# A hybrid decoder layer: activations of the output projections loaded ahead, weights through four tiles, and a new share of dense products per step

## The chip, the cores and the metric

The kernel runs on one core of one Trainium2 chip. The metric is the device time of one launch in microseconds (us), as the median of several runs; lower is better. A second source is one profiled execution, whose trace gives the start and the length of each instruction on the engines: TensorE (PE, with its weight loads as PEld), VectorE (DVE), ScalarE (ACT), GpSimd (POOL) and SyncE (SP, which here only starts transfers).

## The reference

One decoder layer for 2048 tokens of width 1024 in float32. Two recurrent mixers work side by side on the columns of one input projection, their outputs go through one output projection, and a gated convolutional FFN follows.

```python
h = _rmsnorm(x, norm1_w[l])
proj = h @ w_in[l]                          # 2048 HGRN2 columns, 1792 RWKV-7 columns
hg_p, rw_p = proj[..., :HG_COLS], proj[..., HG_COLS:]
q_raw, f_raw, i_raw, g_raw = jnp.split(hg_p, 4, axis=-1)
o_hg = _hgrn2_mixer(q_raw, f_raw, i_raw, g_raw, lower_bounds[l], hg_norm_w[l])
rw_p = rw_p + (_token_shift(rw_p) - rw_p) * rw_shift_mu[l]
r, k, v, wd, ad, gd = jnp.split(rw_p, rw_split, axis=-1)
o_rw = _rwkv7_mixer(r, k, v, wd, ad, gd, ...)
x = x + jnp.concatenate([o_hg, o_rw], axis=-1) @ w_out[l]
x = x + _conv_ffn(_rmsnorm(x, norm2_w[l]), w_up[l], conv_w[l], conv_b[l], w_down[l])
```

HGRN2 has 4 heads of 128, RWKV-7 has 8 heads of 64; both carry a state from token to token. A final RMSNorm ends the layer.

## The kernel before

**Precision.** Each large product is made of three (`mm3`, L269 to 272): both operands are split into a rounded part and a rest, by a cast on ScalarE and a subtraction on VectorE (`split`, L250, for weights; `split_to`, L245, for activations), and the products part·part, part·rest and rest·part are added up.

**Phase 1** covers the input projection, both recurrences and three quarters of the output projection, up to about 1300 us of the trace. The tokens lie in four blocks of 512. Three generators are advanced by one loop when the program is built, and so write one interleaved program:

- `rw_stream` runs RWKV-7 in eight supers (`rw_super(nb, s_)`: block nb, four heads each, numbered here 0 to 7 as 2nb + s_). A super prepares its operands, solves a triangular system per chunk of tokens on VectorE (the tiles E, Ti; L811 to 813) and on TensorE (lv, ZT, RHS, UV), runs the recurrence over chunks and stores its output to DRAM as oT (L949). Its `done["rw1"]` counts prepared supers, whose inputs r, k, v have been read; `done["rw2"]` counts finished ones.
- `hg_stream` runs HGRN2 in sixteen units (`hg_unit(nb, j)`), each of which stores 128 rows of oT (L1089).
- `dense()` is the work that fills TensorE: a list of jobs. Per block there are 30 projections P of 128 columns (eight `mm3` each), and the three output projections O0, O1 and O2 (`out_block`), each of 64 `mm3`, for the blocks 0 to 2. O0 stands behind the projections of block 1, O1 behind those of block 2, O2 behind those of block 3. Block 3's own output projection stands at the start of phase 2 (L1208 to 1281, tile `wacc`).

A step of the loop advances each recurrence to its next `yield`, and then the dense list until it has used up a credit of TICK = 2000 ns, at 648 ns for a projection's `mm3` and 680 for an output projection's:

```python
            for key, g in (("r", rw_), ("h", hg_)):
...
            fill(TICK)
```

The engines run their instructions in the order written, each waiting for its inputs and for free tiles.

**An output projection** O works on 512 tokens in four quarters (i2: 256 tokens; dh: 512 output columns). A quarter has eight weight tiles of 128 by 512, and each serves two `mm3`. A weight tile is loaded by GpSimd's queue into `woraw` (a ring of four tiles, tag wraw), and is split into wh and wl (four tiles each, which the projections' weights share). The activations hh and hl are those of the whole block; O0 and O1 read them from oT in DRAM during their first quarter, one of eight rows of 128 before each weight tile, through two tiles `oraw` (tag sg). O2 has the first 256 tokens ready (`oh`, `ol`) and reads the second 256 in its third quarter. The residual input xh goes through the weight ring in one quarter and through sg in the others. During the last quarter of O0 and O1 the next projections' activations are split into hh and hl (`next_block`).

Before a projection's products, `load(i + 1)` starts the next projection's weights (two of the four split tiles), also if an O job comes in between.

The tags s0, s1 and s2 hold r, k and v of a super (two rows of 512 tokens each), tl holds the low-rank columns of a block.

Of the kernel before, what the change touches and what calls it, by code (L numbers as in the profile page):

```python
# [7 lines left out]
F32 = mybir.dt.float32  # L8
# [10 lines left out]
P = 128  # L19
T = 2048  # L20
D = 1024
KD = D // P
BLK = 512
NBLK = T // BLK
FF = 2816
NFF = FF // P
TICK = 2000.0
# [40 lines left out]
def tile_layer(ctx, tc, consts, x, norm1_w, w_in, hg_lb_logits, hg_norm_w, rw_shift_mu, rw_w0, rw_w2,  # L68
# [5 lines left out]
    dma, store = nc.sync.dma_start, nc.gpsimd.dma_start  # L74
# [171 lines left out]
    def split_to(hi, lo, src):  # L246
        c_ = S.copy(hi, src)
        return c_, V.tensor_sub(lo, src, hi.bitcast(F32))
# [25 lines left out]
    def phase1(c1):  # L274
# [31 lines left out]
        def stg(tag, name, bufs):  # L306
            return sp.tile([P, BLK], F32, tag=tag, name=name, bufs=bufs)
# [68 lines left out]
                ready[k] += 1  # L376
            return f

        def out_block(nb, oh=None, ol=None, then=None):


            for i2 in range(2):
                for dh in range(2):
                    accs = [bank("pj") for _ in range(2)]
                    for k in range(KD):
                        if i2 == 0 and dh == 0 and oh is None:
                            raw = stg("sg", "oraw", 2)
                            dma(raw, oT[nb][k * P:(k + 1) * P, :])
                            split_to(hh[:, k, :], hl[:, k, :], raw)
                        if i2 == 1 and dh == 0 and oh is not None:  # L390
                            raw = stg("sg", "oraw", 2)[:, 0:256]
                            dma(raw, oT[nb][k * P:(k + 1) * P, 256:512])
                            split_to(hh[:, k, 256:512], hl[:, k, 256:512], raw)
                        raw = wp.tile([P, 512], F32, tag="wraw", name="woraw", bufs=4)
                        wload(raw, w_out[0, k * P:(k + 1) * P, dh * 512:dh * 512 + 512])
                        wh, wl = split(wp, raw, [P, 512], "w", 4)
                        if k == KD - 2:
                            inputs = dh == 0 and (i2 == 0) == (oh is None)
                            xh = [wp.tile([P, BLK], F32, tag="wraw", name="xh", bufs=4) if inputs else
                                  stg("sg", "xh", 2) for _ in range(2)]  # L400
                            for q in range(2):
                                t0 = nb * BLK + (i2 * 2 + q) * P
                                dma(xh[q], x[0, t0:t0 + P, dh * 512:dh * 512 + 512])
                        for q in range(2):
                            is_ = slice((i2 * 2 + q) * P, (i2 * 2 + q + 1) * P)
                            lhs = ((hh[:, k, is_], hl[:, k, is_]) if oh is None or i2 == 1 else
                                   (oh[k // 4][:, k % 4, is_], ol[k // 4][:, k % 4, is_]))
                            mm3(accs[q], lhs, (wh, wl), k == 0, k == KD - 1)
                            if i2 == 1 and dh == 1 and q == 1:
                                next_block(then, k)  # L410
                            yield 680
                    for q in range(2):
                        V.tensor_add(xh[q], accs[q], xh[q])
                        r0 = (i2 * 2 + q) * P
                        (nc.gpsimd.dma_start if nb == NBLK - 2 and i2 and dh else dma)(
                            x1d[nb][r0:r0 + P, dh * 512:dh * 512 + 512], xh[q])
# [42 lines left out]
        def split_h(nb, k):  # L459

            src, w = rows[nb][:, :, k * P:(k + 1) * P], vec("n1", k)
            h4, l4 = (t_[:, k, :].rearrange("p (i t) -> p i t", i=4) for t_ in (hh, hl))
            act(h4, src, AF.Copy, scale=w)
            V.scalar_tensor_tensor(l4, src, w, h4.bitcast(F32), ALU.mult, ALU.subtract)

        def next_block(nb, k):

            if nb is not None and nb < NBLK:
                for k_ in ([k - 2] if 2 <= k < KD - 1 else [k - 2, k - 1, k] if k == KD - 1 else []):
                    split_h(nb, k_)  # L470

        def sum_load(m):

# [12 lines left out]
        def o_take(m):  # L486

            def f():
                if m == 0:
                    t_ = xp_.tile([P, 2, 2, 4, 256], F32R, tag="xt", name="ohl", bufs=1)  # L490
                    rows["O"] = [[t_[:, c, i] for i in range(2)] for c in range(2)]
                t_ = wp.tile([P, 2, 256], F32, tag="wraw", name="oraw", bufs=4)
                dma(t_, oT[2][2 * m * P:2 * (m + 1) * P, 0:256].rearrange("(k p) t -> p k t", p=P))
                ks = slice(2 * (m % 2), 2 * (m % 2) + 2)
                for i_ in split_to(rows["O"][0][m // 2][:, ks, :], rows["O"][1][m // 2][:, ks, :], t_):
                    tc.keep_in_program_order(i_)
            return f
# [24 lines left out]
        def dense():  # L522
# [36 lines left out]
            for m in range(2):  # L559
                extra += [(at[3] + 14 + 5 * m, ("E", sum_load(m))), (at[3] + 17 + 5 * m, ("E", sum_make(m)))]  # L560
            extra += [(at[3] + 25 + m, ("W", 2, o_take(m))) for m in range(4)]
            for i, jb in sorted(extra, key=lambda e: e[0], reverse=True):
                jobs.insert(i, jb)
            cols = [jb[1] for jb in jobs if jb[0] == "P"]
# [25 lines left out]
            for n, jb in enumerate(jobs):  # L590
                if jb[0] == "E":
                    jb[1]()
                    continue
                if jb[0] == "A":
                    if jb[1] == 0:
                        banks = spread()
                        ahead = transposed(four_tiles(rows[0]), "n1", lambda: next(banks), to_h)
                    continue
                if jb[0] == "T":
                    turns.append(jb[1])  # L600
                    continue
                if jb[0] in "OW":
                    while done["rw2"] < 2 * jb[1] + 2 or done["hg"] < 4 * jb[1] + 4:
                        yield None
                    if jb[0] == "W":
                        jb[2]()
                    else:
                        yield from (out_block(2, *rows["O"]) if jb[1] == 2 else out_block(jb[1], then=jb[1] + 2))
                    continue
                _, col, ev, cond, fin = jb  # L610
                while not cond():
                    yield None
                load(i)
                ws = loaded.pop(i)
                if i == 0:
                    next(ahead)
                    next(ahead)
                    constants()
                load(i + 1)
                i += 1  # L620
                acc = bank("pj")
                then = jobs[n + 1][1] if jobs[n + 1][0] == "A" else None
                for k in range(KD):
                    wh, wl = ws[k // 4]
                    next(ahead, None)
                    mm3(acc, (wh[:, k % 4, :], wl[:, k % 4, :]), (hh[:, k, :], hl[:, k, :]), k == 0, k == KD - 1)
                    aside = k in (1, 5) and len(turns) > 0
                    if aside:
                        turns.pop(0)()
                    if k == KD - 1:  # L630
                        ev(acc)
                        if fin is not None:
                            fin()
                    next_block(then, k)
                    yield 648 + 436 * aside

        def last_dma(nb):
# [18 lines left out]
        def rw_super(nb, s_):  # L656
# [208 lines left out]
            for e in range(2):  # L865
                r0, c0 = er0(e), col0(1, e)
                act(M[r0:r0 + 64, 0, 1, :, :, 0:64], quv[1][c0:c0 + 64, :, :, 0:64], AF.Copy)
            yield
            yield
            XH = tile_("XH", [2, 9, 64], "XH")  # L870
            V.tensor_copy(XH[:, :, 0, :], Xc[:, 2 * s_:2 * s_ + 2, :])
# [82 lines left out]
        def hg_unit(nb, j):  # L954
# [122 lines left out]
            act(sq, op, AF.Square)  # L1077
            hi, lo = (rp.tile([P, BLK], F32R, tag=tag, name="part") for tag in ("Sf", "VT"))
            split_to(hi, lo, sq)
            yield  # L1080
            yield
            ms = bank("hg")
            add_up(ms, ones, hi, lo)
# [29 lines left out]
        def fill(ns):  # L1113
            nonlocal credit
            credit += ns
            while alive["d"] and credit > 0:
                try:
                    c = next(dn_)
                except StopIteration:
                    alive["d"] = False  # L1120
                    return
                if c is None:
                    credit = 0.0
                    return
                credit -= c

        while any(alive.values()):
            for key, g in (("r", rw_), ("h", hg_)):
                if alive[key]:
                    try:  # L1130
                        next(g)
                    except StopIteration:
                        alive[key] = False
            fill(TICK)


    if "1" in stages:
# [498 lines left out]
```

## Time and profile before

| | us |
|---|---|
| median of 3 runs | 2635.08 |
| lowest and highest | 2632.3, 2636.21 |
| profiled execution | 2639.41 |
| its span in the trace | 2637.6 |

| engine | share of the span |
|---|---|
| PE | 97% |
| PEld | 78% |
| DVE | 75% |
| ACT | 52% |
| POOL | 14% |

In a row of the windows view stand a stretch (us from the span's start), its length, the busy time of each engine with its number of instructions, the granted TensorE clock as a share of full speed (PEclk), the mean busy share of the 16 DMA engines, and what they moved in GB/s. A row of the timeline has start, length, engine, line, operation, output<-inputs, and in brackets the idle time of the engine just before and what ended it. In a view of one tile a row has minimum, median and maximum duration in ns and the first and last start. A name such as `hh L247` is the tile and the line that wrote it; a split has its helper's line, wherever it is called from.

### The profile page before, as it was taken

The numbers are of one execution on the slowest core, as the hardware profiler recorded it, in microseconds if no ns is written. First come the engines' busy times: TensorE is split into PE (matmuls) and PEld (weight loads), VectorE is DVE, ScalarE is ACT, GpSimd is POOL, SyncE is SP. The second block draws the span as 40 slices with busy tenths as digits, with TensorE's granted clock in tenths as the row PEclk, the third lists the DMA queues.
The fourth block names the chain that finished last, engine by engine and source line by source line (L and its number), as shares of the span: only waits on it lengthen the run. The fifth ranks groups of instructions, "written<-read, shape, count | busy, mean of one in ns | idle before, by whom it ended". The sixth has DMA issues, their size and how long they took to land.

```text
span 2637.6 us, 51053 instructions
## 1 busy us (share of the span) xinstructions
PE 2545.3 (97%) x19467; PEld 2046.8 (78%) x19467; DVE 1968.2 (75%) x3744; ACT 1384.5 (52%) x2266; POOL 381.7 (14%) x686
## 2 busy tenths in 40 slices
PE   7999999989999899999899999999999999999998
PEld 6877777767777677777688888887888888888887
DVE  5878676775576765787678799987998887766556
ACT  5566454555446554355466754556554554545444
POOL 6433222212222122222100000000000000000000
PEclk9999999989999999999899999999999999999999
DMA  8846463545655566755574477746764554998655
GB/s 309 236 161 191 159 167 119 148 145 200 195 170 141 168 204 181 252 181 161 193 251 136 130 233 260 235 158 217 243 204 132 170 171 131 333 321 284 200 190 188
DMA packets 380298, 518.98 MB, mean 197 GB/s; under 512 B 114463, under 2 KB 211093, under 8 KB 380053
## 3 DMA queue, kind: packets, MB, share of 16 engines
q1 hardware_dynamic: 325521, 337.38, 40.3%
q0 software_dynamic: 54464, 178.32, 20.9%
q8 instruction: 153, 2.51, 0.4%
q14 instruction: 92, 0.75, 0.1%
q10 hardware_dynamic: 68, 0.02, 0.0%
HBM read 372.99 MB, written 134.22 MB: 192 GB/s over the span
## 4 chain that ended last, share of the span: by engine, by line
PE 53%; issue 7%; DVE 6%; DMA 5%; ACT 4%; POOL 1%; SPq 0%; DVEq 0%; POOLq 0%; ACTq 0%
PE ua L270 5%; PE ua L272 5%; PE ua L271 5%; PE pj L270 3%; PE da L271 3%; PE da L270 3%; PE da L272 3%; PE ud L271 3%; PE pj L271 3%; PE ud L270 3%; PE ud L272 3%; PE pj L272 3%; PE db L271 2%; PE db L272 2%; PE db L270 2%
## 5 line engine op out<-in xcount | busy, mean ns | idle before, releaser
L270 PE MATMUL pj<-hh,wh 128*128 128x512 f32 x960 | 394.6, 411 | 8.2 <-issue 3.4
L272 PE MATMUL pj<-hh,wl 128*128 128x512 f32 x960 | 378.3, 394 | 0.0
L271 PE MATMUL pj<-hl,wh 128*128 128x512 f32 x960 | 377.7, 394 | 0.0
L270 PE MATMUL ua<-Bh,uwh 128*128 128x512 f32 x704 | 276.6, 393 | 2.3 <-ACT m L122 1.2
L272 PE MATMUL ua<-Bh,uwl 128*128 128x512 f32 x704 | 274.9, 391 | 0.0
L271 PE MATMUL ua<-Bl,uwh 128*128 128x512 f32 x704 | 274.5, 390 | 0.0
L270 PEld LDWEIGHTS pj<-hh,wh 128*128 128x128 f32 x960 | 181.2, 189 | 56.6 <-issue 10.1
L272 PEld LDWEIGHTS pj<-hh,wl 128*128 128x128 f32 x960 | 180.8, 188 | 41.0 <-issue 2.0
L271 PEld LDWEIGHTS pj<-hl,wh 128*128 128x128 f32 x960 | 181.5, 189 | 34.6 <-issue 1.6
L254 ACT CAST uwh<-uraw 128x512 fp32r<-128x512 f32 x220 | 134.5, 617 | 131.2 <-PE ua L271 54.7
L255 DVE TENSOR_TENSOR dal<-draw,dah 128x512 fp32r<-128x512 f32 x138 | 95.3, 691 | 108.3 <-ACT dah L254 106.9
L255 DVE TENSOR_TENSOR uwl<-uraw,uwh 128x512 fp32r<-128x512 f32 x220 | 147.4, 686 | 34.1 <-ACT uwh L254 33.8
L254 ACT CAST dah<-draw 128x512 fp32r<-128x512 f32 x138 | 85.7, 621 | 160.8 <-PE da L271 75.9
L270 PEld LDWEIGHTS ua<-Bh,uwh 128*128 128x128 f32 x704 | 132.4, 188 | 32.0 <-ACT m L122 3.8
L272 PEld LDWEIGHTS ua<-Bh,uwl 128*128 128x128 f32 x704 | 132.4, 188 | 27.9 <-DVE uwl L255 0.4
L271 PEld LDWEIGHTS ua<-Bl,uwh 128*128 128x128 f32 x704 | 132.3, 188 | 26.9
L1506 POOL DMA_DIRECT2D gd<-y x2 | 1.1, 542 | 948.8 <-DVE y L1504 948.8
L270 PE MATMUL ud<-Bh,uwh 128*128 128x512 f32 x352 | 138.2, 393 | 0.0
L272 PE MATMUL ud<-Bh,uwl 128*128 128x512 f32 x352 | 137.3, 390 | 0.0
L271 PE MATMUL ud<-Bl,uwh 128*128 128x512 f32 x352 | 137.2, 390 | 0.0
L271 PE MATMUL da<-dbl,dah 128*128 128x512 f32 x332 | 129.6, 390 | 0.3 <-DVE dbl L255 0.3
L272 PE MATMUL da<-dbh,dal 128*128 128x512 f32 x332 | 129.4, 390 | 0.0
(582 smaller groups left out, 6226.7 us busy)
## 6 DMA issues: line engine op xcount, KB each, us to landing
uraw<-in_w_up_dram SPq DMA_DIRECT2D x176, 256.0 KB
woraw<-in_w_out_dram POOLq DMA_DIRECT2D x96, 256.0 KB, 3.5
br<-gd SPq DMA_DIRECT2D x88, 256.0 KB
draw<-Sg SPq DMA_DIRECT2D x88, 256.0 KB
draw<-Tw SPq DMA_DIRECT2D x88, 256.0 KB
gd<-y SPq DMA_DIRECT2D x86, 256.0 KB
Sg<-br SPq DMA_DIRECT2D x72, 256.0 KB
xt<-x1d SPq DMA_DIRECT2D x32, 512.0 KB
```

What stands on the lines that cost most here:

```text
L254: S.copy(hi, src)
L255: V.tensor_sub(lo, src, hi.bitcast(F32))
L270: TE.matmul(acc, lh, rh, start=first, stop=False, skip_group_check=skip)
L271: TE.matmul(acc, lh, rl, start=False, stop=False, skip_group_check=skip)
L272: TE.matmul(acc, ll, rh, start=False, stop=last, skip_group_check=skip)
L1506: (dma if end is None else nc.gpsimd.dma_start)(gd_[2 * h + b][fb * P:(fb + 1) * P, :], ys[0][:, b * BLK:(b + 1) * BLK])
```

## The change

Four things change.

1. A new job "L" stands before the last projection ahead of O0 and of O1. `o_load` starts the loads of all eight rows of oT: six in pairs into the tiles s0, s1, s2, one into tl, one into sg. `next_out` splits them into hh and hl behind the products of that last projection, as soon as the projection has used the old ones (`behind(k)`). For O2, `o_half` loads the second 256 tokens into s0 and s1, and they are split in the second quarter and not in the third.
2. The projection ahead of an O job doesn't load the next projection's weights any more. O0 and O1 do so themselves, behind k = 3 of their last quarter (`ahead`). Until then all four split tiles take O's weights. xh always goes through sg.
3. The credit of a loop step is multiplied by 1.5 while super 3 or 5 lies between its preparation and its end (`done["rw1"]` 4 or 6), by 0.9 once all RWKV-7 inputs of the last block are projected, and else by 1.
4. The last super and the last two HGRN2 units have one `yield` less each.

The number of products, splits and weight loads is as before.

```diff
-        def out_block(nb, oh=None, ol=None, then=None):
+        def out_block(nb, oh=None, ol=None, then=None, ahead=None):
...
-                        if i2 == 0 and dh == 0 and oh is None:
-                            raw = stg("sg", "oraw", 2)
-                            dma(raw, oT[nb][k * P:(k + 1) * P, :])
-                            split_to(hh[:, k, :], hl[:, k, :], raw)
-                        if i2 == 1 and dh == 0 and oh is not None:
-                            raw = stg("sg", "oraw", 2)[:, 0:256]
-                            dma(raw, oT[nb][k * P:(k + 1) * P, 256:512])
-                            split_to(hh[:, k, 256:512], hl[:, k, 256:512], raw)
+                        if i2 == 0 and dh == 1 and oh is not None:
+                            split_to(hh[:, k, 256:512], hl[:, k, 256:512], rows["O2"][k // 4][:, k % 4, :])
...
-                            inputs = dh == 0 and (i2 == 0) == (oh is None)
-                            xh = [wp.tile([P, BLK], F32, tag="wraw", name="xh", bufs=4) if inputs else
-                                  stg("sg", "xh", 2) for _ in range(2)]
+                            xh = [stg("sg", "xh", 2) for _ in range(2)]
...
                             if i2 == 1 and dh == 1 and q == 1:
                                 next_block(then, k)
+                                if k == 3 and ahead is not None:
+                                    ahead()
...
+        def behind(k):
+            return [k - 2] if 2 <= k < KD - 1 else [k - 2, k - 1, k] if k == KD - 1 else []
...
+        def o_load(nb):
+            pieces = []
+            for u in range(3):
+                t_ = sp.tile([P, 2, BLK], F32, tag=f"s{u}", name="opair")
+                dma(t_, oT[nb][2 * u * P:2 * (u + 1) * P, :].rearrange("(k p) t -> p k t", p=P))
+                pieces += [t_[:, 0], t_[:, 1]]
+            for tag, bufs in (("tl", 1), ("sg", 2)):
+                pieces.append(stg(tag, "oraw", bufs))
+                k = len(pieces)
+                dma(pieces[-1], oT[nb][(k - 1) * P:k * P, :])
+            rows[("P", nb)] = pieces
+
+        def o_half(nb):
+            rows["O2"] = []
+            for u in range(2):
+                t_ = sp.tile([P, 4, 256], F32, tag=f"s{u}", name="ohalf")
+                dma(t_, oT[nb][4 * u * P:4 * (u + 1) * P, 256:512].rearrange("(k p) t -> p k t", p=P))
+                rows["O2"].append(t_)
+
+        def next_out(nb, k):
+            for k_ in behind(k):
+                split_to(hh[:, k_, :], hl[:, k_, :], rows[("P", nb)][k_])
...
+            extra += [(len(jobs) - 1, ("L", 2))]
+            extra += [(at[nb] - 2, ("L", nb - 2)) for nb in range(2, NBLK)]
...
-                load(i + 1)
+                if jobs[n + 1][0] != "O":
+                    load(i + 1)
...
+                    if after is not None:
+                        next_out(after, k)
                     yield 648 + 436 * aside
...
-            yield
+            if (nb, s_) < (NBLK - 1, 1):
+                yield
             yield
             XH = tile_("XH", [2, 9, 64], "XH")
...
-            yield
+            if (nb, j) < (NBLK - 1, 2):
+                yield
             yield
             ms = bank("hg")
...
-            fill(TICK)
+            fill(TICK * (0.9 if ready["rw"] == 2 * NBLK else 1.5 if done["rw1"] in (4, 6) and done["rw2"] < done["rw1"] else 1.0))
```

The next rows show the order of ScalarE's instructions where O0 begins (a row is line, operation, output<-input and shape; + of the changed kernel, - of the one before). `hh` is O0's activations, split from `opair` and `oraw`; `wh` is the weights; `Af`, `hX`, `KT` and `hv` belong to HGRN2.

```order
+L254 CAST wh<-woraw 128x512 x2
+L122 ACTIVATE hv<-pj 128x512
+L247 CAST hh<-opair 128x512 x3
+L254 CAST wh<-woraw 128x512
+L247 CAST hh<-opair 128x512
 L122 ACTIVATE hX<-hf 128x256
-L122 ACTIVATE hv<-pj 128x512
 L122 ACTIVATE Af<-hg 32x4x32 x2
 L122 ACTIVATE Af<-A 32x4x32 x4
+L247 CAST hh<-oraw 128x512
 L254 CAST wh<-woraw 128x512
```

Two weight tiles of O0 are now cast first, and the casts of hh from the early tiles follow as a run, ahead of the HGRN2 rows that stood before O0's first weight tile.

SP starts the transfers. Around O0's activations (`oT_143` is block 0's output) the rows before are these; `yo` is a super's output, KBT, Ed and E are the operands of super 3's solve.

```order
L949 DMA oT_144<-yo 128x2x512
L766 DMA KBT<-KBb 32x16x32 x3
L754 DMA Ed<-M 32x16x32 x4
L766 DMA KBT<-KBb 32x16x32 x2
L757 DMA E<-Ed 64x1024 x2
L766 DMA KBT<-KBb 32x16x32 x11
L388 DMA oraw<-oT_143 128x512 x2
L1089 DMA oT_144<-hgg 128x512
L388 DMA oraw<-oT_143 128x512 x4
```

In the changed kernel the rows at the same place are these.

```order
L985 DMA oT_144<-yo 128x2x512
L480 DMA oraw<-oT_143 128x512
L475 DMA opair<-oT_143 128x2x512 x2
L801 DMA KBT<-KBb 32x16x32 x3
L789 DMA Ed<-M 32x16x32 x4
L801 DMA KBT<-KBb 32x16x32 x2
L792 DMA E<-Ed 64x1024 x2
L801 DMA KBT<-KBb 32x16x32 x11
L475 DMA opair<-oT_143 128x2x512
L480 DMA oraw<-oT_143 128x512
L395 DMA xh<-in_x_dram 128x512 x2
```

Three of the five transfers of O0's activations have moved ahead of super 3's KBT, Ed and E loads, and two stand directly behind them.

At the end of phase 1 GpSimd's queue has O2's weight loads and the last stores of the two streams (`hgg` from HGRN2, `yo` from RWKV-7). Before:

```order
L395 DMA woraw<-in_w_out_dram 128x512 x10
L1089 DMA oT_146<-hgg 128x512
L395 DMA woraw<-in_w_out_dram 128x512 x18
L949 DMA oT_146<-yo 128x2x512
L1089 DMA oT_146<-hgg 128x512
```

And in the changed kernel:

```order
L389 DMA woraw<-in_w_out_dram 128x512 x7
L1126 DMA oT_146<-hgg 128x512
L389 DMA woraw<-in_w_out_dram 128x512 x19
L985 DMA oT_146<-yo 128x2x512
L1126 DMA oT_146<-hgg 128x512
L389 DMA woraw<-in_w_out_dram 128x512 x2
```

Two weight tiles now come behind the streams' last stores. On TensorE, 20 products of O2 stand behind the last HGRN2 unit's sums of squares, where 6 stood.

More of the change, by code (lines that the diff above doesn't have):

```diff
@@ L464, in split_h @@
             V.scalar_tensor_tensor(l4, src, w, h4.bitcast(F32), ALU.mult, ALU.subtract)
+        def behind(k):
+            return [k - 2] if 2 <= k < KD - 1 else [k - 2, k - 1, k] if k == KD - 1 else []
         def next_block(nb, k):
             if nb is not None and nb < NBLK:
-                for k_ in ([k - 2] if 2 <= k < KD - 1 else [k - 2, k - 1, k] if k == KD - 1 else []):
+                for k_ in behind(k):
                     split_h(nb, k_)
+        def o_load(nb):
[16 more added lines that the diff above has]
+        def next_out(nb, k):
+            for k_ in behind(k):
+                split_to(hh[:, k_, :], hl[:, k_, :], rows[("P", nb)][k_])
         def sum_load(m):
@@ L607, in dense @@
                     else:
-                        yield from (out_block(2, *rows["O"]) if jb[1] == 2 else out_block(jb[1], then=jb[1] + 2))
+                        yield from (out_block(2, *rows["O"]) if jb[1] == 2 else out_block(jb[1], then=jb[1] + 2, ahead=lambda i=i: load(i)))
+                    continue
+                if jb[0] == "L":
+                    while done["rw1"] < 2 * jb[1] + 4 or done["rw2"] < 2 * jb[1] + 2 or done["hg"] < 4 * jb[1] + 4:
+                        yield None
+                    (o_half if jb[1] == 2 else o_load)(jb[1])
                     continue
                 _, col, ev, cond, fin = jb
+                after = jobs[n + 1][1] if jobs[n + 1][0] == "O" and jobs[n + 1][1] < 2 else None
                 while not cond():
```

## The prediction

> **What bounds the kernel now.** I read the page first: which engine fills the span.
>
> ```profile
> span 2637.6 us, 51053 instructions
> PE 2545.3 (97%) x19467; PEld 2046.8 (78%) x19467; DVE 1968.2 (75%) x3744; ACT 1384.5 (52%) x2266; POOL 381.7 (14%) x686
> ```
>
> TensorE (PE) is busy 97% of 2637.6 us, so this change, which leaves PE's instructions as many as they were, can only give back time in which PE idles or runs at a lower clock. The change touches the three output projections that run beside the recurrences (O0, O1, O2). So I read, second, the windows that hold them, from the preparation of a super's solve (L779) to its gate product (L946), and for O2 to the second half's first products. For comparison the first row is pure projection work, and the third a super of the same kind (super 4) that has only projections beside it.
>
> ```profile
> core 0: us, PE busy (x) PEld busy (x) DVE busy (x) ACT busy (x) POOL busy (x), PEclk, DMA share, GB/s
> 25.00:50.00 25.00, 25.00 (x113) 20.60 (x112) 11.87 (x24) 10.19 (x18) 16.19 (x27) 1.00 0.90 319
> 519.60:632.60 113.00, 101.79 (x1274) 77.53 (x1273) 79.13 (x207) 58.69 (x104) 18.46 (x35) 0.92 0.49 146
> 712.50:810.70 98.20, 93.85 (x1407) 75.96 (x1406) 59.72 (x185) 42.85 (x82) 25.22 (x47) 0.98 0.57 167
> 853.20:958.00 104.80, 97.72 (x1411) 74.68 (x1410) 76.39 (x207) 53.46 (x95) 21.17 (x39) 1.00 0.55 163
> 1196.90:1313.00 116.10, 101.08 (x1278) 78.44 (x1277) 85.17 (x213) 60.17 (x109) 19.41 (x35) 0.93 0.52 165
> ```
>
> The columns that matter are the length, PE busy and PEclk. Lost time is length minus busy, and busy times (1 - clock). O0: 113.0 - 101.8 = 11.2 idle, and 0.08 x 101.8 = 8.1 of clock, 19.3 together. Super 4: 4.4 and 1.9, 6.3. O1: 7.1 and nothing. Last stretch: 15.0 and 7.1, 22.1. A busy row can hide stalls, so I read it a second way by the weight loads: work without gaps has PEld 20.60 in 25, or 0.824. At that rate the four rows hold 94.1, 92.2, 90.6 and 95.2 us of work, and lose **18.9** (O0), **6.0** (super 4), **14.2** (O1) and **20.9** (last). The readings agree but for O1 (7.1 or 14.2).
>
> The Trainium skill, "Trainium Kernel Development and Optimization", Best Practices, judges TensorE by the busy share of its weight loads rather than of its matmuls. By it O1 loses 14.2 and the sum below would be 3 higher; by the busy column alone 4 lower. The trace fits the rule where nothing waits, and can't decide O1.
>
> Third, small windows and PE's timeline show what the loss at O0 is made of.
>
> ```profile
> 535.00:540.00 5.00, 3.99 (x29) 3.51 (x28) 4.80 (x17) 2.40 (x3) 0.54 (x1) 1.00 0.27 79
> 540.00:545.00 5.00, 1.78 (x7) 0.80 (x6) 4.61 (x18) 3.83 (x7) 0.00 (x0) 0.90 0.19 74
> 545.00:550.00 5.00, 3.74 (x129) 3.43 (x130) 5.00 (x17) 2.90 (x5) 0.00 (x0) 0.50 0.22 61
> 560.00:565.00 5.00, 3.04 (x13) 2.20 (x12) 4.28 (x16) 2.48 (x4) 1.07 (x2) 0.95 0.61 206
> 565.00:570.00 5.00, 4.42 (x76) 3.17 (x74) 4.89 (x8) 1.99 (x4) 0.00 (x0) 0.71 0.51 155
> 1196.90:1228.50 31.60, 30.62 (x349) 24.38 (x347) 30.45 (x102) 20.55 (x38) 6.64 (x12) 1.00 0.49 138
> ```
> ```profile
> start us, us, engine line op out<-in xcount [idle before <-releaser]
> 546.26 0.54 PE L1000 MATMUL hg<-hq,hk 128*32 128x32 f32 x22 [2.14 <-DVE hk L957]
> 558.92 0.50 PE L270 MATMUL pj<-wh,hh 128*128 128x512 f32 x1 [1.52 <-ACT hh L247]
> 563.89 0.50 PE L270 MATMUL pj<-wh,hh 128*128 128x512 f32 x1 [1.96 <-ACT hh L247]
> 575.25 0.63 PE L270 MATMUL pj<-wh,hh 128*128 128x512 f32 x1
> 575.68 0.63 PE L271 MATMUL pj<-wl,hh 128*128 128x512 f32 x1
> 1263.06 0.79 PE L270 MATMUL pj<-wh,hh 128*128 128x512 f32 x1 [3.01 <-ACT hh L247]
> 1294.48 0.39 PE L270 MATMUL pj<-wh,hh 128*128 128x512 f32 x1
> 1298.33 0.39 PE L272 MATMUL pj<-wh,hl 128*128 128x512 f32 x1
> 1300.87 1.36 PE L1281 MATMUL wacc<-woh,Bh 128*128 128x512 f32 x4 [2.15 <-ACT Bh L247]
> 1308.36 2.07 PE L1281 MATMUL wacc<-woh,Bl 128*128 128x512 f32 x4 [3.61 <-DVE Bl L248]
> ```
>
> PE waits for `hh`, the split of oT, before O0's products: 1.52, 1.96, and 3.01 us at O2. Around such gaps the clock drops to 0.50 to 0.71, and neighbouring matmuls start 0.43 us apart (575.25, 575.68) where 18 of them, 1294.48 to 1298.33, stand 3.85/17 = 0.227 apart: a product of three is **0.68 us** at full clock. In the same windows VectorE (DVE) is 4.3 to 5.0 of 5 busy: the solve's chain runs there, and O0's splits queue among it.
>
> **The change, part by part.** What an O job must do for its weights and activations:
>
> ```profile
> L395 POOL DMA_DIRECT2D woraw<-in_w_out_dram x96: 537/537/762, 283.9 to 1286.0; - x96
> L254 ACT CAST wh<-woraw x96: 601/619/627, 531.9 to 1290.5; 128x512 fp32r<-128x512 f32 x96
> L255 DVE TENSOR_TENSOR wl<-woraw,wh x96: 655/690/695, 532.6 to 1291.3; 128x512 fp32r<-128x512 f32 x96
> DMA to landing us min/median/max: 2.8/3.5/6.9
> L248 DVE TENSOR_TENSOR hl<-oraw,hh x24: 418/684/693, 548.1 to 1278.0; 128x512 fp32r<-128x512 f32 x16, 128x256 fp32r<-128x256 f32 x8
> ```
>
> 1. *oT loaded ahead and split behind the last projection (O0, O1); second half split a quarter earlier (O2).* The counts stay: 24 subtractions of 0.42 to 0.69 us and as many casts. They only move out of the product's chain, so the `hh` waits and the clock loss that follows them go. SP issues 5 DMAs for them where it issued 8, of the same bytes, now ahead of and behind the super's KBT loads. They wait for the tiles of r, k and v, and a late tile would hold those KBT loads on SP, and the solve behind them. I cost that at nothing: r and k have been read by then, the pair that takes v's tile stands behind the KBT loads, and projections on PE cover the transfers; uncovered, the whole gain of O0's entry (its `hh` waits, 3.5) would go.
>
> 2. *Four weight tiles instead of two.* 96 loads, casts and subtractions as before. Before, the next projection's weights held two of the four split tiles all through O0 and O1: a weight tile's two products (2 x 0.68 = 1.37 us) left just time for one cast and one subtraction (0.62 + 0.69 = 1.31). Now two more lie ahead, and xh leaves the weight ring for `sg`. Its gain is inside the losses below; where its stall goes, the next late thing is DVE (rival 2).
>
> 3. *Thicker steps* (1.5 times the dense work while supers 3 and 5 solve): no instruction added; dense work moves from behind the super to beside its solve.
>
> 4. *Thinner steps at the end* (0.9), and one yield fewer in each of the last three units of the streams: 20 products instead of 6 stand behind the last stream instruction, 14 x 0.68 = 9.6 us. In return the streams end earlier, and phase 2's first loads (waits of 2.15 and 3.61) start under those products.
>
> The sum. Unavoidable loss I take from super 4: 6.0 in 98.2, or 6.1% of length.
> - O0: 18.9 - 0.061 x 113.0 = 12.0. Thicker steps: the 6.9 that remains is lost at a fixed amount per loop step, and half again as much cover in a step should take some half of it, 3 (an estimate; bounds 0 and 6.9). Together **15**; bounds 6 (only the idle beyond super 4's comes back: 11.2 - 4.35 x 113.0/98.2 = 6.2) and 19 (all).
> - O1: 14.2 - 6.4 = 7.8 by weight loads, 0.7 by the busy column; midway 4.3, and thicker steps 3 more: 7.3, taken as **8**, since the weight-load reading is the nearer to O0's kind. Bounds 1 and 14.
> - Last stretch: 20.9 - 7.1 = 13.8. The thinner steps were not seen in any run; they cost between nothing (all 9.6 of tail hides phase 2's loads) and 9.6 (streams as bare as the work taken from them). I take 4, nearer to the lower end because 2.15 + 3.61 = 5.8 of the 9.6 return at the seam: **10**. Bounds 4 and 14.
>
> Sum 15 + 8 + 10 = **33**, bounds 11 and 47. The profiled execution took 2639.4 us, 1.8 more than its span and 4.3 above the median 2635.1 of the runs shown. 2639.4 - 33 = 2606.4 for an execution like it; for the median, 2635.1 - 33 = **2602**. Bounds 2635.1 - 47 = 2588 and 2635.1 - 11 = 2624.
>
> **The rivals.**
>
> 1. *Forecast*: 2602, 0.60.
>
> 2. *VectorE becomes the bound in the solves.* For it: in 545 to 550 it is busy 5.00 of 5, and in super 7's solve 30.45 of 31.60, with PE losing only 1 us there. More weight splits beside a solve would then stretch it by what they cost: an estimate of 12 more products is 6 weight tiles, 6 x 0.69 = 4.1 us, at two supers 8; O2's eight subtractions of 0.42 move into super 7's solve, 3.4 where 1.15 is spare, 2; and the thicker steps' 3 + 3 isn't gained. Against: PE's long waits there are named after ACT's `hh`, and PE loses only 1.0 in super 7's stretch. Time: 33 - 16 = 17, 2618. 0.19.
>
> 3. *All loss above nothing comes back* at O0, and O1's by weight loads: 47, 2588 or less. 0.07.
>
> 4. *It doesn't do what it says*: the early loads land no earlier than they are split, PE waits for the same `hh`. Against: the order has the splits before O's first product. Within 5 us of before, 2635. 0.07.
>
> 5. *Slower: the weight ring starves.* With four tiles, each is reloaded after its own release: issue 0.54, landing 3.5, cast 0.62, subtraction 0.69, together 5.35 us, while four tiles feed 8 products, 8 x 0.687 = 5.5. So at the median landing 0.15 us is to spare. Now wider oT transfers, and 1.5 times the demand of weights during solves, may raise the landing above 3.65; then each round of the ring loses the difference, and 96/4 = 24 rounds pay it: at a landing of 6.0 (the maximum seen is 6.9), 24 x 2.35 = 56, against the 33 of the forecast: +23, 2658. It eats the gain at a landing of 33/24 + 3.65 = 5.0, and decides (slower by 0.2%) from 5.25. For it:
>
> ```profile
> POOL woraw L395 <- DVE wl L255: 152.9, 49, 15.2
> ```
>
> POOL waits 153 us in 49 loads for a free tile: the ring is tight. Against: the DMA share at O0 is 0.49, at O1 0.55, and in 25 to 50 it reached 0.90. 0.07.
>
> The Trainium skill, "DMA: Bandwidth & Descriptors", "Issuing engines are not separate DMA queues", says that transfers started by any engine share the same 16 DMA engines and interleave. By that, oT's loads on SP and woraw's on POOL would slow one another; the trace's spare share leaves this rival small, and no run here shows them together yet.
>
> **How the numbers follow.** Likeliest is 1, so 2602. Range: from case 3's 2588 to 2627, which is the bound 2624 and 3 for the scatter of the runs (2632.3 to 2636.2); it takes in cases 1 and 2 (0.79) and the upper part of 3. Left out: 4, 5 and the rest of 3. The measurement can tell about 0.2%, 5.3 us. Faster by more: cases 1, 2, 3: 0.86; same: case 4: 0.07; slower: case 5: 0.07.
>
> **What would show it.** Casts of `hh` from the early tiles before O's first product; no wait of 1.5 to 3 us for `hh`; clock 1.00 from 535 to 580, not 0.50 (step 1). `wl` ahead of its product by two tiles, landing median still below 4 (2; above 5: rival 5). Solve stretches of supers 3 and 5 not longer than before though thicker (3; DVE at 95% or more and longer: rival 2). Twenty products after the last stream instruction, and no 3.61 us for `Bl` (4). The forecast is wrong if the clock stays low at O0 without the waits, since then 8 of O0's 15 were never theirs.

## The result, and the profile after

The changed kernel takes 2615.14 us (median; 2611.61 to 2618.16) beside 2635.64 for the kernel before. The ratio is 0.9918, with a 95% interval of 0.9905 to 0.9932: 0.8% faster, 20.5 us by the medians, where 33 were forecast (2602; range 2588 to 2627). Two executions in a far slower state of the chip, one of the repeat of factor 1 (4906.17 us) and one of the kernel before (3577.9), are left out of the times and ratios below.

First the head of the page of the changed kernel.

```profile
span 2612.8 us, 51006 instructions
PE 2536.2 (97%) x19467; PEld 2044.4 (78%) x19467; DVE 1966.4 (75%) x3744; ACT 1381.1 (53%) x2266; POOL 380.8 (15%) x686
```

PE has the same 19467 instructions, and the span is 24.8 us shorter (2637.6 before). To see where, I divided both traces at the same points of the program: from the solve preparation of super 3 to that of super 4 (this holds O0 and the dense work behind it), of super 5 to 6 (O1), from the end of that to the first product of phase 2 (this holds supers 6 and 7 and O2), and the 25 us behind that. The third stretch is also shown from super 7's solve preparation on alone. The thinner steps leave work undone ahead of super 7 (1627 instructions of PE where there were 1640), so the row from there on holds a dozen more in the changed kernel (1442 for 1430). The other stretches up to the seam hold the same products, so their lengths can be compared. The windows of the kernel before:

```profile
core 0: us, PE busy (x) PEld busy (x) DVE busy (x) ACT busy (x) POOL busy (x), PEclk, DMA share, GB/s
519.60:712.50 192.90, 178.79 (x1665) 137.71 (x1664) 125.25 (x281) 102.55 (x168) 43.56 (x82) 0.96 0.58 177
853.20:1048.00 194.80, 183.08 (x1833) 140.29 (x1832) 128.94 (x293) 103.17 (x170) 47.16 (x88) 1.00 0.60 184
1048.00:1300.90 252.90, 237.90 (x3067) 188.71 (x3065) 185.86 (x458) 122.06 (x205) 56.78 (x106) 0.99 0.62 190
1187.30:1300.90 113.60, 102.63 (x1430) 81.12 (x1428) 82.02 (x213) 59.04 (x106) 19.86 (x38) 0.97 0.53 160
1300.90:1325.90 25.00, 20.95 (x78) 16.20 (x79) 12.23 (x20) 9.46 (x17) 2.24 (x4) 0.80 0.76 257
```

And of the changed kernel:

```profile
520.70:702.60 181.90, 172.08 (x1666) 134.93 (x1665) 126.44 (x281) 101.90 (x168) 43.71 (x82) 0.97 0.59 180
843.50:1030.40 186.90, 180.14 (x1833) 141.75 (x1832) 128.89 (x293) 103.10 (x170) 46.91 (x88) 0.99 0.60 185
1030.40:1278.60 248.20, 238.75 (x3067) 190.12 (x3066) 183.35 (x459) 122.67 (x208) 57.86 (x107) 0.99 0.63 195
1167.50:1278.60 111.10, 106.11 (x1442) 84.63 (x1441) 79.66 (x214) 59.86 (x109) 22.20 (x41) 0.97 0.54 162
1278.60:1303.60 25.00, 24.50 (x107) 19.63 (x106) 13.99 (x23) 9.54 (x17) 1.09 (x2) 1.00 0.87 286
```

By length O0 gives 192.9 - 181.9 = 11.0, O1 194.8 - 186.9 = 7.9, and the stretch with O2 only 252.9 - 248.2 = 4.7. In the 25 us behind the seam, as the place where phase 2 begins is called here, PE does more at the full clock (24.50 at 1.00, where it was 20.95 at 0.80). From the seam to its last product the trace is 2.4 us shorter, which is less than executions of the same code differ by there (up to 6.6 us, see below). In the other stretches, whose code is nearly unchanged, the changed kernel is 1.3 us longer (520.7 for 519.6 us ahead of O0, and 140.9 for 140.7 between O0 and O1).

Of the waits for `hh` at the three entries none is left. What is late in their place at O0 stands in the timelines of the changed kernel, of VectorE and then of PE (start, length, instruction, idle time before it and its releaser):

```profile
572.05 0.66 DVE L255 TENSOR_TENSOR wl<-woraw,wh 128x512 fp32r<-128x512 f32 x1
572.74 2.85 DVE L858 STREAM_TRANSPOSE TTs<-TZ 32x512 f32<-32x512 f32 x4
575.53 1.24 DVE L407 TENSOR_TENSOR xh<-pj,xh 128x512 f32<-128x512 f32 x2
```
```profile
572.19 0.59 PE L865 MATMUL rw<-TZ,M 32*32 32x32 f32 x44
576.32 0.76 PE L270 MATMUL pj<-wh,hh 128*128 128x512 f32 x1 [3.54 <-DVE xh L407]
576.88 0.63 PE L271 MATMUL pj<-wl,hh 128*128 128x512 f32 x1
577.31 0.63 PE L272 MATMUL pj<-wh,hl 128*128 128x512 f32 x1
```

The additions that empty O0's accumulators (`xh` L407) stand on VectorE's queue behind 2.85 us of the solve's transposes. PE waits 3.54 us for an accumulator, and its next matmuls start 0.43 us apart, about twice the 0.227 us of the full clock. Two windows of the same kernel show how the clock stands there, and the first that the dip at the entry of the solve has not gone either:

```profile
545.00:550.00 5.00, 3.06 (x9) 1.64 (x9) 4.65 (x17) 4.82 (x8) 0.00 (x0) 0.54 0.15 52
575.00:580.00 5.00, 3.68 (x10) 2.95 (x11) 4.00 (x8) 0.63 (x2) 1.61 (x3) 0.66 0.50 169
```

### The profile page after: what moved, and what is told of

It reads as the page before. It is cut to its first block, busy times and chain, and to the rows that moved or that the text cites. A ratio compares the mean times of both kernels' runs of the same rounds, so it can differ in the third digit from the quotient of the medians.

```text
span 2612.8 us, 51006 instructions
## 1 busy us (share of the span) xinstructions
PE 2536.2 (97%) x19467; PEld 2044.4 (78%) x19467; DVE 1966.4 (75%) x3744; ACT 1381.1 (53%) x2266; POOL 380.8 (15%) x686
```

## The experiments

All times are medians, and the ratios are to the kernel before. **A** is the theory of the prediction's sum: each part is worth its term. **B** is its second rival: VectorE bounds the solves, so that thicker steps are paid back. The third question is the seam between the phases: do the thin steps pay there or cost?

**One factor each.** The first kernel has factor 1 in every step:

```diff
-            fill(TICK * (0.9 if ready["rw"] == 2 * NBLK else 1.5 if done["rw1"] in (4, 6) and done["rw2"] < done["rw1"] else 1.0))
+            fill(TICK)
```

> The changed kernel with every loop step at its full credit (factor 1 throughout); early loads, four weight tiles and the missing yields stay. Theory A (the prediction's terms): the thick steps are worth 3 + 3 us and the thin ones cost 4, so about 2 us slower than the changed kernel: near 2617 where that was 2615. Theory B (VectorE bounds the solves, so thick steps are paid back): the thick steps are worth nothing or cost, and the thin steps too: 2608 to 2615.

Measured: 2608.23, ratio 0.9893 (0.9878 to 0.9907), and in a repeat 2605.45 (three executions), 0.9887 (0.987 to 0.9904). Faster than the changed kernel, as B said and A did not. Which of the two factors did it, and whether by B's mechanism, the next two runs ask.

The second keeps 0.9 and drops 1.5:

```diff
+            fill(TICK * (0.9 if ready["rw"] == 2 * NBLK else 1.0))
```

> The changed kernel without the factor 1.5 (0.9 at the end stays). Theory A: 6 us slower than the changed kernel, 2621. Theory B: within 2 us of it or faster, 2610 to 2616, and the stretches of supers 3 and 5 about 22 and 27 us shorter, the dense stretches behind them as much longer.

Measured: 2614.1, 0.9917 (0.9903 to 0.9931): no difference that can be told from the changed kernel, again as B said, while A's 2621 missed. From the solve's preparation to the gate product supers 3 and 5 are 30 and 31 us shorter (105.3 and 100.4 for 135.4 and 131.8), more than the 22 and 27 of B.

The third keeps 1.5 and drops 0.9:

```diff
+            fill(TICK * (1.5 if done["rw1"] in (4, 6) and done["rw2"] < done["rw1"] else 1.0))
```

> The changed kernel without the factor 0.9 (1.5 beside supers 3 and 5 stays). Theory A: the thin steps cost 4, so 4 us faster than the changed kernel, 2611. Rival: what the tail of products hides at the seam to phase 2 (waits of 2.1 and 3.6 us before, and a clock of 0.50 there) is worth more than what the streams lose: 3 to 6 us slower, 2618 to 2621, with waits before the first wacc products.

Measured: 2600.82, 0.9864 (0.9847 to 0.9881), and in a repeat

> The kernel without the thin steps once more, beside the next one on the same chip: 2601 (the first time 2600.8), within 3 us.

2604.45, 0.9879 (0.9865 to 0.9893). The thin steps cost, and far more than the 4 us of A: the two ratios average 0.9872, which is 0.0046 x 2635 = 12 us below the changed kernel's 0.9918 (with the intervals, some 8 to 17). So the first kernel was faster than the changed one by its full steps at the end, and not because 1.5 is paid back, as B had it. The windows of this kernel at super 7 and at the seam show part of it.

```profile
1168.30:1270.40 102.10, 100.68 (x1430) 78.93 (x1429) 79.57 (x213) 59.60 (x107) 20.21 (x38) 1.00 0.56 168
1270.40:1295.40 25.00, 23.54 (x101) 18.50 (x100) 13.96 (x23) 10.56 (x19) 1.82 (x3) 1.00 0.86 291
```

102.1 us where the changed kernel needs 111.1. A part of these 9.0 us is the work left undone ahead of super 7. With that stretch the row holds the same 3067 instructions of PE as the changed kernel's:

```profile
1028.90:1270.40 241.50, 236.11 (x3067) 186.45 (x3066) 183.35 (x458) 122.66 (x206) 57.09 (x106) 1.00 0.65 199
```

241.5 where the changed kernel needs 248.2: 6.7 us (6.8 in the repeat, 241.4). The two profiled executions differ by 8.4 us over the whole span (2612.8 and 2604.4), so this stretch holds most of what the traces can show; the medians say more, and where the rest of the 12 lies is open. From super 7 on PE idles 1.4 us and the clock is 1.00; in the changed kernel it idles 5.0 at 0.97. The changed kernel's windows show one of the places:

```profile
1215.00:1220.00 5.00, 3.08 (x110) 2.48 (x112) 4.94 (x13) 3.14 (x9) 1.09 (x3) 0.78 0.40 125
1220.00:1225.00 5.00, 5.00 (x64) 4.49 (x61) 4.84 (x14) 1.21 (x3) 1.06 (x2) 0.54 0.61 202
```

Beside the solve's small products too little dense work is left, PE is busy 3.08 of 5, and the clock then falls to 0.54. The kernel without thin steps has a clock of 1.00 there.

**What mended the seam.** It wasn't the thin steps alone, since without them PE is also busy 23.54 of the 25 us behind it. The fourth kernel puts the three yields back, and has no thin steps:

```diff
-            if (nb, s_) < (NBLK - 1, 1):
-                yield
+            yield
...
-            if (nb, j) < (NBLK - 1, 2):
-                yield
+            yield
```

> The changed kernel without the factor 0.9 and with the three yields put back; factor 1.5, early loads and four tiles stay. Theory A (the three yields hide the seam: without them the streams end five products earlier, so phase 2's first loads get cover): 4 to 6 us slower than the kernel without the thin steps, near 2606, with waits for Bh and Bl of 2 to 4 us at the first wacc products. Rival (the early loads alone mended the seam): no difference, 2601.

Measured: 2615.1, 0.992 (0.9907 to 0.9934): 13 us behind the kernel without the thin steps. Its windows and its timeline of PE have the old seam:

```profile
1166.00:1273.70 107.70, 101.62 (x1429) 79.41 (x1427) 79.42 (x213) 59.30 (x106) 19.70 (x38) 1.00 0.54 159
1273.70:1298.70 25.00, 20.11 (x75) 15.79 (x76) 11.42 (x19) 8.78 (x16) 2.32 (x4) 0.86 0.73 251
```
```profile
1273.74 1.20 PE L1316 MATMUL wacc<-woh,Bh 128*128 128x512 f32 x4 [2.13 <-ACT Bh L247]
...
1280.98 2.08 PE L1316 MATMUL wacc<-woh,Bl 128*128 128x512 f32 x4 [4.24 <-DVE Bl L248]
```

So it is the missing yields that hide the seam: without them and with full steps, 11 products stand behind the last HGRN2 sums instead of 6, and the longest of these waits in the kernel without thin steps is 0.96 us. The thin steps bought cover that was there already; whether they would pay with the yields in place no run shows. The profiled execution with the yields is the fastest of its six (2610.99), and only 4.8 and 6.4 us longer in its span than the two without (2609.2 for 2604.4 and 2602.8). The stretch up to the seam, which ends with the first wait, holds some 5 of them (107.7 against 102.1 and, in the repeat, 102.7). What the second wait costs can't be told: from the seam to the last product executions of the same code differ by up to 6.6 us (1322.1 to 1328.7 in ten executions with this seam mended), and with both waits it is 1327.7.

**Half as thin.**

```diff
+            fill(TICK * (0.95 if ready["rw"] == 2 * NBLK else 1.5 if done["rw1"] in (4, 6) and done["rw2"] < done["rw1"] else 1.0))
```

> The changed kernel with 0.95 in place of 0.9 at the end. Theory A (each product taken from beside the streams costs what it takes at the tail, nothing is hidden by it once the yields have covered the seam): half of the cost of 0.9, 2607 to 2610. Rival (the cost comes from the clock that drops once a gap is long enough): nothing yet at 0.95, 2601 to 2604, clock 1.00 through super 7's stretch.

Measured: 2608.88, 0.9908 (0.9895 to 0.9921), half of the cost or more, as A expects. Its window does not show it so clearly:

```profile
1170.70:1274.50 103.80, 102.12 (x1435) 80.50 (x1434) 79.25 (x214) 60.44 (x109) 21.20 (x40) 1.00 0.58 171
```

103.8 against 102.1 is 1.7 us (with the stretch ahead of it, and so the same products, 242.8 against 241.5, or 1.3), and the clock is 1.00, which is what the rival expected of the profile. A's rule fits the traces in size: 14 products stand behind the last HGRN2 sums here, 11 with full steps and 20 with 0.9, and at 0.68 us the 3 and the 9 more are 2.0 and 6.1 us, beside the 1.3 and 6.7 of the traces. But the medians say 4 to 8 for 0.95, and the ratios 9.5. That 0.95 costs is measured; by what mechanism is open.

**Thicker and less thick.** Both on the kernel without thin steps:

```diff
-1.5 if done["rw1"] in (4, 6)
+2.0 if done["rw1"] in (4, 6)
```

> The changed kernel without the factor 0.9, and with 2.0 in place of 1.5 beside supers 3 and 5. Theory A (a step loses a fixed amount, so thicker steps gain): 2 to 5 us faster than with 1.5, 2596 to 2599. Theory B (VectorE bounds the solves): slower than with 1.5 by 2 to 8 us, 2603 to 2609, with VectorE over 95% busy in longer solves.

Measured: 2663.61, 1.0107 (1.0091 to 1.0122): 61 us slower than with 1.5. Neither theory had this size. The window of this kernel in super 5, and the timeline of PE with the last product before and the next one behind it:

```profile
900.00:920.00 20.00, 10.04 (x163) 8.20 (x164) 18.56 (x70) 7.96 (x15) 0.00 (x0) 0.57 0.01 4
```
```profile
892.56 0.39 PE L272 MATMUL pj<-wh,hl 128*128 128x512 f32 x1
...
902.77 0.63 PE L1036 MATMUL hg<-hX 128*32 128x16 f32 x32 [2.88 <-DVE hX L1017]
...
911.69 0.48 PE L826 MATMUL rw<-UV,M 64*64 64x64 f32 x4 [4.08 <-ACT UV L122]
...
914.64 0.79 PE L270 MATMUL pj<-wh,hh 128*128 128x512 f32 x1
```

For 22 us no dense product stands there: the list had run ahead to the load of O1's activations, which waits for super 5 to be prepared. In the program as built nine steps of the loop found the list waiting for a stream and wrote no dense work (three of them here, five at the load of O2's activations), and for the last seven it was used up. The streams run bare, PE is busy half of the time, and the clock is 0.57. The bound from above on the factor is the supply of dense work, not VectorE alone, busy as it is (18.56 of 20).

```diff
-1.5 if done["rw1"] in (4, 6)
+1.25 if done["rw1"] in (4, 6)
```

> The kernel without the thin steps with 1.25 in place of 1.5 beside supers 3 and 5. Factor 1 gave 2607 to 2608, 1.5 gave 2601 to 2604, 2.0 gave 2664 with 15 steps that found no dense work. If the gain is by the step: midway, 2605. If 1.5 already runs short of work anywhere: 1.25 is faster, 2598 to 2601.

Measured: 2598.5, 0.9867 (0.9852 to 0.9883), the same as with 1.5 (0.9864 and 0.9879). The repeat of factor 1 was run for the same question:

> The kernel with factor 1 throughout once more. Theory A: the thick steps are worth 6, so 2607, 6 us behind the kernel without the thin steps. Theory B, and the sums of the two profiled executions (0.5 us apart over both projections): no difference, 2602 to 2605.

The two ratios with factor 1 average 0.989, those with 1.5 0.9872: the thick steps are worth about 5 us, with an uncertainty of some 4. Beside thin steps they were worth nothing that could be told (0.9918 with them, 0.9917 without, uncertain by 5). The lengths of the stretches agree at O0 (183.5 with factor 1 in both executions, 181.0 with 1.5: 2.5 us) and say nothing at O1 (187.6 and 186.8 against 189.5 and 184.8).

**Early loads and four tiles.** Loads and splits inside the output projections as before (also O2's, in its third quarter, and xh through the weight ring), all else as in the changed kernel:

```diff
-                        if i2 == 0 and dh == 1 and oh is not None:
-                            split_to(hh[:, k, 256:512], hl[:, k, 256:512], rows["O2"][k // 4][:, k % 4, :])
+                        if i2 == 0 and dh == 0 and oh is None:
+                            raw = stg("sg", "oraw", 2)
+                            dma(raw, oT[nb][k * P:(k + 1) * P, :])
+                            split_to(hh[:, k, :], hl[:, k, :], raw)
...
-            extra += [(len(jobs) - 1, ("L", 2))]
-            extra += [(at[nb] - 2, ("L", nb - 2)) for nb in range(2, NBLK)]
```

> The changed kernel with O's activations loaded and split inside the output projections as before (and xh of that quarter through the weight ring as before); four weight tiles, factors and yields stay. Theory A: the early loads are the largest part (entry waits of 3.5, 2.1 and 3.0 us and the clock that drops around them): 10 to 15 us slower than the changed kernel, 2625 to 2630, with waits for hh L247 back at all three projections. Theory B: the splits cost VectorE the same wherever they stand, so no more than the 8.6 us of named waits returns, 2617 to 2623.

Measured: 2633.41, 0.999 (0.9978 to 1.0002): without the early loads all of the gain is gone, 19 us, more than either theory had. By the stretches 6.8 at O0 (188.7), 6.2 at O1 (193.1) and 9.5 at O2 (120.6). Waits for `hh` are back at O0 (0.9 us) and O2 (3.9); at O1, where A expected them too, they are 0.2. The view of PE's waits over that last stretch (us in total, times, longest) begins

```profile
PE pj L270 <- ACT hh L247: 3.9, 4, 1.5
PE pj L270 <- ACT wh L254: 2.9, 2, 2.6
```

So the named waits are only a part of what the late loads cost, and the rest of the mechanism isn't shown.

The early loads alone on the kernel before (factor 1 throughout, all yields, two weight tiles):

> The kernel before with the early loads alone: two split tiles, factor 1 throughout, all yields in place (xh goes through sg). Theory A (the parts add up: thick steps 5, tiles 4, yields 12, early loads the rest of 32): 10 to 13 us faster than before, 2622 to 2625, with the seam's waits of 2 and 4 us still there and hh waits gone. Rival (early loads pay only where steps and tiles let O use them): under 6 us faster, 2629 or more.

Measured: 2621.43, 0.9954 (0.9941 to 0.9967), 12 us faster, with the seam as before and no wait for `hh` named at any of the three; as large as A's sum had it. The timeline of PE in this kernel:

```profile
1287.60 2.07 PE L1315 MATMUL wacc<-woh,Bl 128*128 128x512 f32 x4 [5.38 <-DVE Bl L248]
```

Last the weight tiles, on the kernel without thin steps:

```diff
-                if jobs[n + 1][0] != "O":
-                    load(i + 1)
+                load(i + 1)
```

> The kernel without the thin steps, and with the next projection's weights loaded ahead of O0 and O1 again, so that O's weights have two of the four split tiles. Theory A (two tiles leave a product pair's 1.37 us for a cast and a subtraction of 1.31, and any delay on VectorE reaches TensorE): 3 to 8 us slower than with four, 2606 to 2611, with waits for wl L255. Rival (the splits keep up, or VectorE is late either way): within 2 us, 2601 to 2605.

Measured: 2611.07, 0.9919 (0.9905 to 0.9932): 12 us slower than with four tiles (0.9872), above the upper end of A. The stretches show 0.8 at O0 and 2.1 to 6.8 at O1 (two executions with four tiles); the window of O1 with two tiles:

```profile
842.50:1034.10 191.60, 186.04 (x1833) 144.57 (x1832) 130.53 (x293) 103.75 (x170) 46.88 (x88) 0.97 0.58 180
```

PE is busier (186.0 against 180.4 with four tiles) in a stretch that is 2.1 us longer, at 0.97 instead of 0.99 of the clock. It isn't `wl` that it waits for, as A had it: PE's waits in this stretch begin with

```profile
PE pj L270 <- DVE hgg L370: 1.9, 1, 1.9
PE rw L950 <- DVE XH L957: 1.1, 1, 1.1
```

and in the whole run the products of TensorE wait for `wl` once, for 0.3 us, where with four tiles it is 2.8 us in 6 waits. That two tiles cost is measured; the mechanism that A gave is not what the trace names, and the right one is open.

## Why the prediction was right, and where its sizes were off

The direction, the range and the main mechanism held: the three output projections lost time at their entries, and loading and splitting ahead gives a part of it back. The size didn't: 33 were forecast, and 24.8 by the span and 20.5 by the medians came.

1. *Early loads.* As expected, the `hh` waits are gone. Alone they give 12 us; taken out of the changed kernel they cost 19. This is the largest part, and the prediction put it so. It also expected a clock of 1.00 from 535 to 580; the trace has 0.54 at 545 to 550 and 0.66 at 575 to 580. That is in part the sign by which the prediction said it would be wrong (a clock that stays low at O0 without the waits): over the stretch of O0 the clock rose only from 0.96 to 0.97, and PE's busy time times the missing share fell from 7.2 to 5.2 us, which is 2 of the 8 that it had counted as clock (the clock of a row is rounded to 0.01, which leaves some 2 us open).

2. *O0: 15 forecast, 11.0 measured by length.* What was missed is the new wait of 3.54 us for `xh` and the half clock behind it (0.34 x 3.68 = 1.3 us): together 4.8. That is near the difference of 4, but it isn't shown to be it. With factor 1 the waits for `xh` are 0.6 us (in their place stand 3.0 for `ZT` and 2.0 for `hgg`), with 1.25 none is named, and the stretch is no shorter (183.5 and 182.7). The second rival's mechanism (VectorE's queue in the solve) is what stands there, at one place and not throughout.

3. *O1: 8 forecast, 7.9 measured.* The two readings of O1 had disagreed before: 7.8 to gain by the weight loads, 0.7 by the busy column. The 7.9 lies at the first, though executions of one code differ by 4.7 here (189.5 and 184.8). Over the whole stretch, now that both traces are there, the busy column (idle, and busy times (1 - clock)) gives 11.7 before and 6.8 + 1.8 = 8.6 after, a gain of 3.1. The weight-load reading (length minus PEld/0.824) gives 24.5 and 14.9, a gain of 9.6, of which 1.8 is that the weight loads of the same products took 1.46 us longer; the length fell by 7.9, nearer to the second. The Trainium skill, "Trainium Kernel Development and Optimization", Best Practices, prefers the busy share of weight loads to that of matmuls; here the trace agrees with it (7.8 by the weight loads and 0.7 by the busy column, against 7.9).

4. *Thick steps: 3 + 3 forecast, about 5 measured, uncertain by 4* (kernels without thin steps; 2.5 by length at O0; nothing that can be told beside thin steps). The sign named for them, solve stretches not longer than before, did not come: super 3 takes 135.4 us from the solve's preparation to the gate product where it took 113.0, and super 5 131.8 where it took 104.8. These rows hold 135 and 128 more instructions of PE, so their lengths couldn't show the gain. VectorE is busy 92.0 and 92.1 us of them, about 0.7, not the 95% of rival 2.

5. *The last stretch is the term that was mis-sized most: 10 forecast, 4.7 measured by length up to the seam.* The prediction said of the thinner steps "I take 4, nearer to the lower end because 2.15 + 3.61 = 5.8 of the 9.6 return at the seam". The runs showed that the seam belongs to the missing yields (back with them: waits of 2.13 and 4.24, 13 us by the medians), and that nothing was left for the thin steps to win. Of the 14 products moved to the tail the yields moved 5 and the thin steps 9. These cost 6.7 us in the traces, about what they take (9 x 0.68 = 6.1), and 12 (8 to 17) by the ratios. Without the thin steps the stretch gains 11.4 (252.9 to 241.5), where the prediction had 13.8 to give back. What is gained behind the seam (2.4) can't be told from the scatter. With 6.7 in place of 4 the sum would have been 30, with 12 it would have been 25; the 4 missing at O0 are a second, smaller error, whose cause is open.

6. *The weight ring (rival 5) did not starve.* In the view of the tile `woraw` of the changed kernel the landing is

```profile
DMA to landing us min/median/max: 2.8/3.7/6.8
```

3.7 where it was 3.5, far from the 5.0 from which that rival would have eaten the gain. The page "DMA: Bandwidth & Descriptors" of the Trainium skill, under "Issuing engines are not separate DMA queues", has such transfers share the engines; a cost beyond the 0.2 us can't be seen in these rows.

That the parts add up was only partly tested: early loads 12, tiles 12, yields 13 and thick steps 5 are 42, while the kernel with all four and no thin steps gains 0.0128 x 2635 = 34. The early loads were measured alone, and the other three were taken out of a kernel that has all the rest, where a part also counts what it lends to the others. Each figure is uncertain by 3 to 5, so the difference of 8 is not clear of noise.

A version that beats both kernels came out: the change without the thin steps, 2600.82 and 2604.45 (0.9864 and 0.9879), and with 1.25 in place of 1.5, 2598.5 (0.9867).

## What to carry to other kernels

When several edits aim at one wait, ask which of them still finds it there: a wait that two edits remove is paid for once, and the second edit's price stays. Work that covers another engine's latency should be moved as a supply that can run out: factors of 1.25 and 1.5 did no harm and gained about 5 us, uncertain by 4; 2.0 found no work in 16 steps and lost 61 us; and 0.9 left PE idle beside a solve and cost 12. Where a named wait goes, look at who shares the queue of its releaser: the next late instruction was an addition behind 2.85 us of transposes on the same engine.

## What was not expected of the hardware

The clock fell without a long idle time: in the changed kernel PE is busy 3.08 of 5 us (1215 to 1220), with no wait over 0.87 us, and the granted clock is 0.54 in the next 5. With the factor 2.0 it was 0.57 over 20 us in which PE was busy half of the time with small products, between gaps of mostly 1.3 to 2.9 us and one of 4.08. After the single gap of 3.54 us at 572.8 the matmuls ran 0.43 us apart for about 3 us.
